# Placing the split weight tiles of a two-layer decoder trunk at 22 patterns of address distances, with four tiles of each part instead of five

## The chip, the cores and the metric

The kernel runs on one core of one Trainium2 chip. The metric is the device time of one execution in microseconds (us), as the median of several runs. Beside it there is the span of one profiled execution, from its first to its last instruction.

## The reference

A trunk of two layers runs over one sequence of 256 tokens with 2048 channels. Layer 0 mixes tokens by causal pooling, layer 1 by attention with 16 heads. Each layer ends with a gated feed-forward part of inner width 5632. Scale, shift and gate of every part come from a conditioning vector.

```python
def conv_ffn(h, w_up, conv_w, conv_b, w_down):
    u = h @ w_up                          # 2048 -> 2 * 5632
    u = causal_depthwise_conv3(u, conv_w) + conv_b
    val, gate = jnp.split(u, 2, axis=-1)
    return (jax.nn.silu(gate) * val) @ w_down

for i in range(DEPTH):                    # DEPTH = 2
    sh1, sc1, g1, sh2, sc2, g2 = jnp.split(silu(c) @ w_ada[i] + b_ada[i], 6)
    h = modulate(rmsnorm(x, norm_g[i, 0]), sh1, sc1)
    y = pool_mixer(h, ...) if i % 2 == 0 else moba_attention(h, w_qkv, w_o, rel_table)
    x = x + g1 * y
    h = modulate(rmsnorm(x, norm_g[i, 1]), sh2, sc2)
    x = x + g2 * conv_ffn(h, w_up[i], conv_w[i], conv_b[i], w_down[i])
return rmsnorm(x, final_g)
```

All data are float32.

## The kernel before

Every large weight matrix is read once, as 328 blocks of 512 rows by 512 columns, which the code calls steps. A step's block lands in one `raw` tile of [128, 2048] float32, one of five. The step has two halves of 1024 columns of that tile. For each half `w_use` has ScalarE (ACT) copy the weights into a `hi` tile of the rounded type float32r, and VectorE (DVE) subtract, `lo = w - hi`. There are HB = 5 `hi` and 5 `lo` tiles. The activations are split in the same way once (`h` for the up and the query, key and value products, `act` for the down products, `o` for the attention's output), 256 columns of rounded values beside 256 columns of remainders.

The products of a half are put out LAG = 3 halves after its split: `w_use` appends the half to `pending`, and `run_half` takes the oldest one when more than LAG are pending. The function `products` in `group_T` makes three matmuls for each 128 x 128 block of weights: `hi` by the rounded activations, `hi` by the remainders, `lo` by the rounded activations. In all of them the weights are the stationary operand (loaded by LDWEIGHTS) and the 256 columns of activations move. So a half has 4 x 2 x 3 = 24 matmuls and a step 48. Only the value projection (`v_group`) turns the roles round: there `h` is stationary and 512 columns of `hi` or `lo` move, 24 matmuls in a step. The counts are 176 steps for `w_up` (the tiles `uv` and `ug`, 8448 matmuls), 88 for `w_down` (`d`, 4224), 16 each for `k` and `q` (768 each), 16 for `v` (384), 16 for `w_o` (`wo`, 768): 14,976 matmuls with 256 columns and 384 with 512.

The first 200 us go to the conditioning vectors of the first layer (`ws` tiles, summed on DVE and TensorE) and to the pooling. The other conditioning matrices (`wa` tiles) are summed on DVE in between the steps. From event 200 on, TensorE, DVE and ACT keep the order of the program; before that a planner orders them.

Of one partition's memory the kernel takes nearly all. In the layout of the kernel before, the tile `h` starts at byte 36,864, and `act` and `o` tiles start at 156,672 and whole multiples of 8192 after it: both are multiples of 128. The `raw` tiles start at 72,640, the `hi` tiles at 113,600, the `lo` tiles at 134,080, one behind the other in steps of 8192 or 4096: all of these are 64 bytes past a multiple of 128. So in all matmuls of the steps the two operands' addresses differ by 64 bytes modulo 128, and the three operands of DVE's subtraction do not differ modulo 4096. The constants in front of the `raw` tiles set this: `starts` has room for 48 floats, of which 33 are used, and the small table `rel` lies behind the `lo` tiles.

Of the kernel before, what the change touches and what calls it, by code (L numbers as in the profile page):

```python
# [9 lines left out]
F32 = mybir.dt.float32  # L10
F32R = mybir.dt.float32r
# [6 lines left out]
P = 128  # L18
# [3 lines left out]
BUCKETS = 32  # L22
# [3 lines left out]
def bucket_starts():  # L26

    exact = BUCKETS // 2

    def bucket(n):  # L30
        if n < exact:
            return n
        big = exact + int(math.log(n / exact) / math.log(MAX_DIST / exact) * (BUCKETS - exact) + 1e-9)
        return min(big, BUCKETS - 1)

    of = [bucket(n) for n in range(4 * MAX_DIST)]
    return [next((n for n, b in enumerate(of) if b >= want), 1 << 20) for want in range(BUCKETS)]
# [19 lines left out]
def trunk(ctx: ExitStack, tc: tile.TileContext, x, c, norm_g, w_ada, b_ada, pool_w, pool_scale, w_qkv, w_o,  # L57
# [3 lines left out]
    _, S, D = x.shape  # L61
# [4 lines left out]
    H = rel_table.shape[1]  # L66
    NT = S // P
    SCALE = float(P) ** -0.5
    C = 512
# [3 lines left out]
    const = ctx.enter_context(tc.tile_pool(name="const", bufs=1))  # L73
    wp = ctx.enter_context(tc.tile_pool(name="wp", bufs=1))
# [2 lines left out]
    dram = ctx.enter_context(tc.tile_pool(name="dram", bufs=1, space=bass.MemoryType.DRAM))  # L77

    PE_BLOCKS = ((2, 5, 8, 11, 14), (3, 7, 11, 15), (2, 4, 6, 9, 11, 13, 15), (2, 5, 7, 10, 13, 15), ())
    RAW, HB, LAG, T4, PRIO = 5, 5, 3, 6, 1000  # L80

    def raw_tile(name):
        return wp.tile([P, 4 * C], F32, tag="raw", name=name, bufs=RAW)
# [4 lines left out]
    def aux(name):  # L88
        return psum.tile([P, C], F32, tag="aux", name=name, bufs=2)

    def wt(shape, tag, bufs, name, dt=F32):
        return work.tile(shape, dt, tag=tag, bufs=bufs, name=name)

    rel = wt([BUCKETS, H], "rel", 1, "rel")


    ident = const.tile([P, P], F32, name="ident")
# [310 lines left out]
    steps = []  # L408
# [259 lines left out]
    def bias_rows():  # L668

        starts = bucket_starts() + [1 << 20]  # L670
        st = const.tile([P, 48], F32, name="starts")[:, :BUCKETS + 1]
        for b, v in enumerate(starts):
            nc.gpsimd.memset(st[:, b:b + 1], float(v))
        nc.gpsimd.dma_start(rel, rel_table)
        e = wt([H, S + P], "t4", T4, "bias_e")
        nc.gpsimd.memset(e, NEG)
        for t in range(NT):
            ni = wt([P, 1], "st", 8, f"ni{t}", I32)
            nc.gpsimd.iota(ni, pattern=[[0, 1]], base=t * P, channel_multiplier=1)
            n = wt([P, 1], "st", 8, f"nf{t}")  # L680
            ve.tensor_copy(n, ni)
            ge = wt([P, BUCKETS + 1], "oh", 2, f"ge{t}")
            ve.tensor_scalar(ge, st, n, None, op0=ALU.is_le)
            oh = wt([P, BUCKETS + 1], "oh", 2, f"oh{t}")
            ve.tensor_tensor(oh[:, :BUCKETS], ge[:, :BUCKETS], ge[:, 1:], op=ALU.subtract)
            ps = aux(f"ohp{t}")
            pe.transpose(ps[:BUCKETS, :P], oh[:, :BUCKETS], ident)
            ohT = wt([BUCKETS, P], "vec", 4, f"ohT{t}")
            ve.tensor_copy(ohT, ps[:BUCKETS, :P])
            ps2 = aux(f"ohe{t}")  # L690
            pe.matmul(ps2[:H, :P], rel, ohT, start=True, stop=True)
            ve.tensor_copy(e[:, P - 1 + t * P:P - 1 + (t + 1) * P], ps2[:H, :P])
        nc.gpsimd.dma_start(bias_dram, e)
# [273 lines left out]
    def run_half():  # L967
        i, half, hi, lo = pending.pop(0)
        steps[i][3](half, hi, lo)
        if half == 1:  # L970
            for f in hooks.get(i, ()):
                f()
        h_next = ahead.pop(0) if ahead else None
        if h_next:
            h_next()
        else:
            run_tasks(2 if len(tasks) > MANY else 1)
        for _ in range(2):
            if folds:
                folds.pop(0)()  # L980
        for d in list(deferred):
            d[0] -= 1
            if d[0] <= 0:
                deferred.remove(d)
                d[1]()

    def w_use(i):
        def use(r):
            for half in range(2):
                hi = wp.tile([P, 2 * C], F32R, tag="hi", name=f"hi{i}_{half}", bufs=HB)  # L990
                lo = wp.tile([P, 2 * C], F32R, tag="lo", name=f"lo{i}_{half}", bufs=HB)
                src = r[:, half * 2 * C:(half + 1) * 2 * C]
                ac.activation(hi, src, AF.Copy)
                ve.tensor_tensor(lo, src, hi.bitcast(F32), op=ALU.subtract)
                pending.append((i, half) + tuple(t.rearrange("p (k c) -> p k c", k=2) for t in (hi, lo)))
                if len(pending) > LAG:
                    run_half()
        return use
# [47 lines left out]
    i = 0  # L1046
# [86 lines left out]
```

## Time and profile before

| | us |
|---|---|
| median of 3 runs | 2127.83 |
| lowest and highest of them | 2125.51, 2127.96 |
| the profiled execution's own time | 2123.99 |
| its span | 2121.9 |

The profiled execution was a little faster than all three of the runs, and its span leaves out 2.1 us of its own time. The mean granted TensorE clock of the execution was 0.984 of full speed. In the views, PE is the matmuls of TensorE, PEld its weight loads, DVE VectorE, ACT ScalarE. Matmuls overlap in the views, since one begins before the one ahead of it has drained, so the time that a matmul costs is the distance from its start to the next one's, and not its duration.

### The profile page before, as it was taken

The page shows a single profiled execution, that of the slowest core. Times are in us where ns is not written, and L with a number is a line of the kernel's source. Part 1 is how long each engine was busy: PE and PEld are TensorE (multiplying, and loading weights), DVE is VectorE, ACT ScalarE, POOL GpSimd, SP SyncE. Part 2 cuts the span into 40 slices and gives each one's busy share as a digit, 9 for nine tenths or more (in the row PEclk, how much of TensorE's full clock was granted, in tenths as well). Part 3 has the DMA queues.
Part 4 walks back from the last instruction along what each step waited for, and adds up shares of the span by engine and source line. Part 5 has one row for each costly group of instructions (what it writes and reads, how often), then busy time and mean ns, then how long its engine had stood idle before and what let it go on. Part 6 is the DMA issues. An engine that isn't in the chain of part 4 may idle for free.

```text
span 2121.9 us, 38504 instructions
## 1 busy us (share of the span) xinstructions
PE 2066.2 (97%) x16292; PEld 1963.9 (93%) x16292; DVE 1643.3 (77%) x2023; ACT 959.2 (45%) x1206; POOL 12.0 (1%) x64
## 2 busy tenths in 40 slices
PE   6888999999999999999999999999999999999998
PEld 2435999999999999999999999999999999999998
DVE  6877799799879998997787878779775666556655
ACT  3113633566354445444544444445443454434443
POOL 1000000000000000000000000000000000000000
PEclk9889999999999999999999999999999999999999
DMA  9999999565998988896888888578765555555551
GB/s 357 333 348 345 335 334 320 198 197 181 348 332 292 358 314 308 304 326 213 307 294 310 295 310 302 190 259 282 278 233 179 190 179 189 196 180 188 192 179 60
DMA packets 236445, 558.78 MB, mean 263 GB/s; under 512 B 9272, under 2 KB 9592, under 8 KB 221680
## 3 DMA queue, kind: packets, MB, share of 16 engines
q1 hardware_dynamic: 234800, 553.17, 74.5%
q8 instruction: 127, 2.08, 0.4%
q0 software_dynamic: 896, 2.49, 0.4%
q10 hardware_dynamic: 576, 0.67, 0.1%
q14 instruction: 46, 0.38, 0.0%
HBM read 554.17 MB, written 2.12 MB: 262 GB/s over the span
## 4 chain that ended last, share of the span: by engine, by line
PE 95%; DVE 2%; DMA 2%; ACT 1%; issue 1%; ACTq 0%; SPq 0%; DVEq 0%
PE uv L50 24%; PE ug L50 23%; PE d L50 23%; PE k L50 4%; PE wo L50 4%; PE q L50 4%; PE v L50 4%; PE row L50 2%; PE pp L50 2%; PE mods L50 1%; DVE accs L50 1%; DVE pool_room L50 1%; DMA w<-in_w_up_dram 1%; DMA ws<-in_w_ada_dram 1%; PE sc L50 0%
## 5 line engine op out<-in xcount | busy, mean ns | idle before, releaser
L50 DVE TENSOR_TENSOR lo<-w,hi 128x1024 fp32r<-128x1024 f32 x656 | 793.9, 1222 | 320.7 <-ACT hi L50 319.7
L50 ACT ACTIVATE hi<-w 128x1024 fp32r<-128x1024 f32 x656 | 682.3, 1057 | 671.9 <-PE d L50 215.8
L50 PE MATMUL uv<-h,hi 128*128 128x256 f32 x2816 | 503.8, 281 | 4.2 <-ACT h L50 4.1
L50 PE MATMUL ug<-h,hi 128*128 128x256 f32 x2816 | 501.6, 280 | 0.2 <-ACT hi L50 0.2
L50 PE MATMUL d<-act,hi 128*128 128x256 f32 x2816 | 497.5, 280 | 0.0
L50 PEld LDWEIGHTS uv<-h,hi 128*128 128x128 f32 x2816 | 433.2, 189 | 5.2 <-ACT h L50 4.9
L50 PEld LDWEIGHTS ug<-h,hi 128*128 128x128 f32 x2816 | 431.3, 188 | 0.5 <-ACT hi L50 0.5
L50 PEld LDWEIGHTS d<-act,hi 128*128 128x128 f32 x2816 | 428.9, 187 | 0.0
L50 PE MATMUL uv<-h,lo 128*128 128x256 f32 x1408 | 394.1, 280 | 0.0
L50 PE MATMUL ug<-h,lo 128*128 128x256 f32 x1408 | 393.2, 279 | 0.0
L50 PE MATMUL d<-act,lo 128*128 128x256 f32 x1408 | 390.9, 279 | 0.0
L50 PEld LDWEIGHTS uv<-h,lo 128*128 128x128 f32 x1408 | 265.8, 189 | 0.0
L50 PEld LDWEIGHTS ug<-h,lo 128*128 128x128 f32 x1408 | 264.8, 188 | 0.0
L50 PEld LDWEIGHTS d<-act,lo 128*128 128x128 f32 x1408 | 263.5, 188 | 0.0
L50 DVE SCALAR_TENSOR_TENSOR acc<-wa,cond,acc 128x2048 f32<-128x2048 f32 x105 | 246.3, 2346 | 3.5 <-DMA wa<-in_w_ada_dram 3.3
L50 DVE SCALAR_TENSOR_TENSOR accs<-ws,cond,accs 128x512 f32<-128x512 f32 (+1 forms) x179 | 157.4, 882 | 23.3 <-DMA ws<-in_w_ada_dram 12.5
L50 PE MATMUL k<-h,hi 128*128 128x256 f32 x512 | 94.0, 285 | 1.1 <-ACT h L50 1.1
L50 PE MATMUL q<-h,hi 128*128 128x256 f32 x512 | 91.4, 280 | 0.0
L50 PE MATMUL wo<-o,hi 128*128 128x256 f32 x512 | 91.1, 280 | 0.0
L50 PE MATMUL row<-ws,cond 128*1 128x512 f32 x152 | 79.5, 647 | 10.3 <-DMA ws<-in_w_ada_dram 10.3
L50 PEld LDWEIGHTS k<-h,hi 128*128 128x128 f32 x512 | 79.9, 190 | 2.3 <-ACT h L50 1.4
L50 PE MATMUL v<-hi,h 128*128 128x512 f32 x256 | 80.4, 395 | 0.0
(157 smaller groups left out, 1751.7 us busy)
## 6 DMA issues: line engine op xcount, KB each, us to landing
w<-in_w_up_dram SPq DMA_DIRECT2D x176, 1024.0 KB, 5.2
wa<-in_w_ada_dram SPq DMA_DIRECT2D x112, 1024.0 KB, 6.0
w<-in_w_down_dram SPq DMA_DIRECT2D x88, 1024.0 KB, 5.1
ws<-in_w_ada_dram SPq DMA_DIRECT2D x56, 1024.0 KB, 9.0
w<-in_w_qkv_dram SPq DMA_DIRECT2D x48, 1024.0 KB, 5.9
ws<-in_w_ada_dram SPq DMA_DIRECT2D x48, 512.0 KB, 5.8
w<-in_w_o_dram SPq DMA_DIRECT2D x16, 1024.0 KB, 5.3
pw<-in_pool_w_dram SPq DMA_DIRECT2D x4, 1024.0 KB, 9.1
```

The source lines that it names most:

```text
L50: ins = call(*args, **kwargs)
```

## The change

Each `hi` and `lo` tile gets 32 floats (128 bytes) more, and the 1024 columns in use begin 0, 32, 64 or 96 bytes into it. Which of them is set by the step's column block of 512: `n`, the block's number modulo 22, chooses a row of `SHIFTS`, which has four entries, for `hi` and `lo` of the first half and `hi` and `lo` of the second. Rows 0 to 15 are all combinations of 0 and 64. Rows 16 and 17 are 96 and 32 everywhere, rows 18 to 21 are mixtures of 96 with 64 and of 32 with 96. The tiles' names get a letter from a to v for the row. `HB` goes from 5 to 4 and `LAG` from 3 to 2. The table `rel` moves from behind the `lo` tiles to the constants, with 24 floats of room, and `starts` has 33 floats instead of 48.

```diff
-    RAW, HB, LAG, T4, PRIO = 5, 5, 3, 6, 1000
+    RAW, HB, LAG, T4, PRIO = 5, 4, 2, 6, 1000
+    SHIFTS = [tuple(64 * ((n >> b) & 1) for b in range(4)) for n in range(16)]
+    SHIFTS += [(96, 96, 96, 96), (32, 32, 32, 32), (96, 64, 96, 64), (64, 96, 64, 96), (32, 96, 32, 96), (96, 32, 96, 32)]
...
-    rel = wt([BUCKETS, H], "rel", 1, "rel")
...
-        st = const.tile([P, 48], F32, name="starts")[:, :BUCKETS + 1]
+        st = const.tile([P, BUCKETS + 1], F32, name="starts")
...
+        rel = const.tile([BUCKETS, H + 8], F32, name="rel")[:, :H]
...
-                hi = wp.tile([P, 2 * C], F32R, tag="hi", name=f"hi{i}_{half}", bufs=HB)
-                lo = wp.tile([P, 2 * C], F32R, tag="lo", name=f"lo{i}_{half}", bufs=HB)
+                n = steps[i][2] // C % len(SHIFTS)
+                hi, lo = (wp.tile([P, 2 * C + 32], F32R, tag=w, name=f"{w}{'abcdefghijklmnopqrstuv'[n]}{i}_{half}",
+                                  bufs=HB)[:, s // 4:s // 4 + 2 * C]
+                          for w, s in zip(("hi", "lo"), SHIFTS[n][2 * half:2 * half + 2]))
```

## Rows read from the trace of the kernel before

**Rows 1.** The page: busy time by engine, then the granted TensorE clock in 40 slices.

```profile
PE 2066.2 (97%) x16292; PEld 1963.9 (93%) x16292; DVE 1643.3 (77%) x2023; ACT 959.2 (45%) x1206; POOL 12.0 (1%) x64
...
PEclk9889999999999999999999999999999999999999
```

**Rows 2.** The page: the chain that ended last, shares of the span by engine.

```profile
PE 95%; DVE 2%; DMA 2%; ACT 1%; issue 1%; ACTq 0%; SPq 0%; DVEq 0%
```

**Rows 3.** The chain in order of time: start us, length us, what, instructions.

```profile
173.25 7.10 PE pp L50 x32
...
527.29 90.45 PE d L50 x768
...
1098.79 11.19 PE v L50 x48
...
1813.61 90.45 PE d L50 x768
1904.07 22.61 PE uv L50 x192
```

**Rows 4.** Two stretches of down products: length, busy us by engine, clock, DMA.

```profile
527.00:617.00 90.00, 90.00 (x767) 90.00 (x766) 73.94 (x57) 42.37 (x54) 0.00 (x0) 1.00 0.92 330
1820.00:1900.00 80.00, 80.00 (x681) 80.00 (x681) 41.87 (x44) 31.60 (x31) 0.00 (x0) 1.00 0.57 187
```

**Rows 5.** The chain in two short stretches of the attention.

```profile
1063.96 0.66 PE pt L50 x6
1064.62 2.73 PE q L50 x24
...
1068.65 2.83 PE q L50 x24
...
1190.47 2.73 PE k L50 x24
```

**Rows 6.** TensorE in order of time, value to key products: start us, length us.

```profile
982.19 0.40 PE L50 MATMUL k<-h,hi 128*128 128x256 f32 x2
982.42 0.28 PE L50 MATMUL k<-h,lo 128*128 128x256 f32 x1
982.55 0.40 PE L50 MATMUL k<-h,hi 128*128 128x256 f32 x2
982.78 0.28 PE L50 MATMUL k<-h,lo 128*128 128x256 f32 x1
982.90 0.40 PE L50 MATMUL k<-h,hi 128*128 128x256 f32 x2
```

**Rows 7.** One-column matmuls in order of time, each with its weight load.

```profile
1353.26 1.93 PE L50 MATMUL ms<-mean_c,sq 128*128 128x1 f32 x16
```

**Rows 8.** Groups by shape, DVE and ACT: busy us, mean ns, idle before.

```profile
L50 DVE TENSOR_TENSOR lo<-w,hi 128x1024 fp32r<-128x1024 f32 x656 | 793.9, 1222 | 320.7 <-ACT hi L50 319.7
...
L50 DVE TENSOR_TENSOR val<-gate,val 128x1024 f32<-128x1024 f32 x22 | 26.8, 1220 | 1.5 <-ACT gate L50 1.4
...
L50 DVE TENSOR_TENSOR pool_room<-pool_room,inv 128x1024 f32<-128x1024 f32 x4 | 4.9, 1219 | 0.0
...
L50 ACT ACTIVATE hi<-w 128x1024 fp32r<-128x1024 f32 x656 | 682.3, 1057 | 671.9 <-PE d L50 215.8 <-PE ug L50 176.9 <-PE uv L50 173.5
...
L50 ACT ACTIVATE sq<-xT 128x1024 f32<-128x1024 f32 x4 | 4.2, 1053 | 28.6 <-DVE xT L50 28.6
```

**Rows 9.** What TensorE waited for: us in total, times, longest us.

```profile
PE ug L50 <- ACT hi L50: 0.2, 1, 0.2
```

**Rows 10.** ACT, DVE and TensorE in order of time, around one half of `wo`.

```profile
1321.66 1.06 ACT L50 ACTIVATE hi<-w 128x1024 fp32r<-128x1024 f32 x1 [1.72 <-PE wo L50]
...
1321.95 1.22 DVE L50 TENSOR_TENSOR lo<-w,hi 128x1024 fp32r<-128x1024 f32 x1
...
1325.12 0.40 PE L50 MATMUL wo<-o,hi 128*128 128x256 f32 x2
```

## The prediction

> **What bounds the kernel now.** I read the page first. TensorE is busy 97% of the span at full granted clock nearly throughout [rows 1], and the chain that ended last is 95% TensorE [rows 2]. Since busy time of overlapping matmuls says little, the chain in order of time comes next, for its pieces give the distance from matmul to matmul: 768 down products in 90.45 us, 192 up products in 22.61 us [rows 3], both 117.8 ns each. The 14,976 matmuls with 256 columns take 14,976 x 117.8 = 1764 us of the 2121.9, so one nanosecond more or less on each is worth 15 us.
>
> Is 117.8 ns set by something that the change touches? The two stretches of down products have DVE busy 82% and 52% of the time and the DMA share at 0.92 and 0.57, and 767 matmuls in 90 us and 681 in 80 are the same distance [rows 4]. So it is set inside TensorE. There are two marks to hold it against. One-column matmuls, where the weight load alone sets the pace, follow each other at about (1.93 - 0.25) / 15 = 112 ns, with 0.25 us off for the last one's own length, an estimate [rows 7]. And in two stretches of 24 matmuls, on the same operands at the same distance of addresses, the matmuls are faster: 2.73 us where the next half takes 2.83 [rows 5], which is 4.2 ns less on each. Both come after short transposes, the first visibly so. So the matmul's own reading and the weight load beside it get in each other's way, by an amount that depends on how the two stand in time to each other, and a stream that has once begun at one pace keeps it. The value products, with 512 columns, take 11.19 / 48 = 233.1 ns [rows 3], where 512 columns at 2.4 GHz would take 213.3: a loss of 20 ns against 117.8 - 106.7 = 11.1 ns with 256 columns. The plain float32 matmuls of the pooling, 7.10 / 32 = 222 ns for 256 columns [rows 3], run at half the column rate and show no sign of a loss that could be told apart. That is all the trace holds: every matmul of the steps has its operands 64 bytes apart modulo 128, so no row shows another distance.
>
> **The change, part by part.** First the addresses that it makes. `starts` shrinks from 192 bytes to 160 (33 floats, in units of 32 bytes) and `rel` adds 96, so `raw` moves up by 64 to 72,704, a multiple of 128. Tiles of 4224 bytes are 33 x 128, so `hi` and `lo` without a shift start at multiples of 128, as `h`, `act` and `o` still do. A shift is thus the distance itself. The row of shifts is the column block's number modulo 22: up products use all 22 rows (384 matmuls each), down, query and output products rows 0 to 3, key products 4 to 7, value products 8 to 11. Counting `hi` twice and `lo` once in each triple, 5344 of the 14,976 matmuls keep the 64 bytes, 7712 have 0, and 1920 have 32 or 96. In halves that hold 6624 matmuls, 2208 triples, `hi` and `lo` have different shifts, so that the distance changes twice in each triple: 4416 changes.
>
> *DVE and ACT.* The subtraction, all operands at one address modulo 128, takes 1222 ns, the gate's product of two tiles at one address modulo 128 takes 1220, and the pooling's product, whose operands lie 64 bytes apart, 1219; ACT's copy takes 1057, its squaring from a tile 64 bytes off 1053 [rows 8]. These differ by less than 1% over the distances that occur, and both engines stand beside TensorE's work. Cost 0; were 1% added to the 794 and 682 us, the idle time of the two would take it in.
>
> *Tiles and lag.* With four tiles a split waits until the products of four halves before are through, not five: it can start one half, 24 x 117.8 = 2.83 us, later, and nothing else holds it. Behind a copy that waits on ACT stand the convolution's and the gate's tasks, and DVE's subtraction waits for it; TensorE waits last. The cover now: TensorE has waited for a split only 0.2 us in all [rows 9]. From the start of each half's first product and the end of its subtraction I find, in the last 596 of the 656 halves, 13 with less than 2.83 us between them, the least 1.62. All shortfalls added, neighbours counted once, make 5.8 us: the upper end. But most of the 13 began late for a load or for work before them on DVE, and such a split does not move. The clearest that does: its copy waits for TensorE and starts at 1321.66, the subtraction ends at 1323.17, and the product begins at 1325.12 [rows 10], so 1.95 us of cover against 2.83, a loss of 0.9. I take 1 us, range 0 to 6. The load behind a split is late by the same 2.83 us at most; five `raw` tiles with the DMA share at 0.57 to 0.92 [rows 4] cover that. The moved table costs nothing: the same transfer on the same queue, long before it is used.
>
> *A new distance that stays.* For 7712 matmuls at 0 and 1920 at 32 or 96, the trace bounds the price from two sides: the shorter pace of [rows 5], -4.2 ns, and a loss as large as that of the value products on a 256-column matmul, 106.7 + 20 = 126.7, so +8.9 ns. On 9632 matmuls that is -40 to +86 us. I take 0, because 117.8 is what all entries but two fell into, after interruptions of every kind.
>
> *Distances that change within a triple.* The nearest row is the passage from value to key products, where operands change roles: the first triple takes 982.19 to 982.55, 0.36 us, the one after it 0.35 [rows 6]. At that resolution a change costs 0 to 7 ns. I take the half, 3.5 ns: 4416 x 3.5 = 15 us, range 0 to 31.
>
> The sum: 1 + 0 + 15 + 0 = 16 us. On the profiled execution that is 2124.0 + 16 = 2140 us. The median of the runs shown is 3.8 us above that execution, and I forecast the median: 2127.8 + 16 = 2144 us, 0.8% slower.
>
> The Trainium skill speaks against any effect of the distance: its page "SBUF — State Buffer", section "Who interferes with whom", gives TensorE two independent read ports, one for the moving operand and one for the weight load, and says that it never waits on anyone. By that only the 1 us for the tiles would be left, 2129 us; the trace does not bear it out fully, since two speeds stand side by side on the same addresses [rows 5]. Its page "TensorE: Matmul & The Clock Gate", section "Back-to-back issue gap", has 262 cycles for 256 columns, an estimate of 109 ns; the trace's 117.8 does not agree, so there is a loss that an address could lengthen or shorten.
>
> **The rivals.** *The distance does nothing.* The loss may be one of time alone: the two speeds on equal addresses [rows 5] speak for that, and so does that the steps' distances are constant and the speed nevertheless is not. Then 2127.8 + 1 = 2129 us, within the bound of 0.2% (4 us), which is about what a measurement can tell here from no change. Against it: the interference is between two reads of one memory.
>
> *Distance 0 or a mixture leads into the shorter pace.* The pace that saves 4.2 ns exists [rows 5]. If distance 0 alone leads to it, 7712 x 4.2 = 32 us go: 2097 us, or 2112 with the 15 us of changes; if all streams fall into it, 62 us, 2067. It becomes faster than before from about (16 + 4) / 4.2 ns = 4800 matmuls on if the changes cost their 15 us. Against it: it is rare, 2 stretches of 24.
>
> *Distance 0 is a bad one.* If a weight load at the moving operand's own address modulo 128 loses as much as the value products do, 7712 x 8.9 = 69 us come on top: 2144 + 69 = 2213. The down products would show it most, as they use rows 0 to 3 alone.
>
> **How the numbers follow.** Changes within a triple cost something, up to the bound of 31 us and with small losses at new distances: 0.45, with a range of its own from 2133 to 2165. Distance 0 bad, in part or wholly, 2165 to 2213: 0.12. Nothing from the distance: 0.16. The shorter pace: 0.27. So slower 0.57, same 0.16, faster 0.27. The range leaves out the deeper third of the faster case, below 2085, and the end of the bad one, above 2200.
>
> **What would show it.** The letters in the tiles' names give each row of shifts its own lines, so pieces of the chain such as 192 matmuls of one up block compare directly with 22.61 us. Right would be: rows a, d, m and p (one distance in a half) near 117.8 ns, rows with unequal `hi` and `lo`, most of all s to v, some 2 ns above. Waits of TensorE for `hi` or `lo` should stay under 6 us in all. DVE's 1222 and ACT's 1057 ns should stand for all letters. What would make me wrong: a block at 113 ns, down products off 117.8 ns at all, or a DVE that is slower at some distance and so late for TensorE.

## The result, and the profile after

The changed kernel takes 2137.9 us (median of 4 runs, 2134.46 to 2140.51), the kernel before beside it 2127.1 (4 runs, 2125.51 to 2127.96): a ratio of 1.0051 with an interval of [1.0033, 1.0068], 10.8 us slower. The forecast was 2144 us, 16 us slower. So direction and size fit, but the sum behind them doesn't: the term that was to bring 15 us brings nothing, and the one put at 1 us brings ten.

The page of the kernel after: busy time by engine, the clock, and four of its groups (busy us, mean ns, idle before).

```profile
PE 2074.7 (97%) x16292; PEld 1967.8 (92%) x16292; DVE 1643.2 (77%) x2023; ACT 959.5 (45%) x1206; POOL 12.0 (1%) x64
...
PEclk8888999999999999999999999999999999999999
...
L50 PE MATMUL d<-act,hia 128*128 128x256 f32 x704 | 126.8, 282 | 0.6 <-ACT hia L50 0.6
...
L50 PE MATMUL d<-act,hid 128*128 128x256 f32 x704 | 124.2, 280 | 0.0
L50 DVE TENSOR_TENSOR loa<-w,hia 128x1024 fp32r<-128x1024 f32 x76 | 91.7, 1222 | 42.1 <-ACT hia L50 41.9
...
L50 ACT ACTIVATE hia<-w 128x1024 fp32r<-128x1024 f32 x76 | 79.3, 1057 | 91.1 <-PE d L50 42.8
```

DVE and ACT work as in [rows 8], 1222 and 1057 ns. TensorE is still busy all the time as in [rows 1], and the down products of letters a and d differ by 2.6 us of busy time over the same 704 matmuls. A busy time of overlapping matmuls can't say what that is worth; the chain in order of time can (start us, length us, what, instructions):

```profile
1262.12 2.26 DVE acc L50
1264.38 1.15 DVE lol L50
...
1265.57 5.83 PE v L50 x24
...
1646.57 22.63 PE uv L50 x192
1669.20 21.76 PE ug L50 x192
...
1713.42 22.55 PE ug L50 x192
...
1826.52 90.80 PE d L50 x768
...
1940.04 23.01 PE ug L50 x192
...
2031.02 22.41 PE ug L50 x192
```

Each piece of 192 matmuls is one up block, and so one row of shifts; against the 22.61 us of [rows 3] these are e 22.63, p 21.76, q 22.55, t 23.01 and v 22.41: from 113.3 to 119.8 ns where everything used to take 117.8. So the distance between the operands' addresses does set TensorE's pace, and both ways. Yet the 768 down products (rows a to d) take 90.80 us instead of 90.45, almost the same, because their four rows in part make up for each other.

That can be seen with every matmul's start taken from the trace. The table gives the mean distance from start to start in the halves whose `hi` and `lo` shifts are the given ones, over all letters:

```
hi, lo shift, bytes   0,0     0,64    64,0    64,64   32,32   96,96   32,96   96,32   64,96   96,64
ns                    119.14  117.60  117.40  115.45  119.09  117.24  118.84  116.65  119.0   118.21
```

Distance 0 costs 1.4 ns against the 117.77 of before, distance 64 gives back 2.3, and all 256-column matmuls of the steps together have 117.87. The 115.45 is a mean of two: of the 80 such halves that the records show whole, 39 stand at 113.3, 38 at 117.3 to 119, and three between.

What TensorE waits for on account of a split (us in total, times, longest us), which was one wait of 0.2 us before [rows 9]:

```profile
PE k L50 <- DVE loh L50: 1.4, 2, 1.2
...
PE d L50 <- DVE lob L50: 1.2, 2, 0.9
...
PE d L50 <- DVE loa L50: 1.1, 1, 1.1
PE v L50 <- DVE loj L50: 0.9, 1, 0.9
PE v L50 <- DVE lok L50: 0.9, 1, 0.9
PE v L50 <- DVE lol L50: 0.8, 1, 0.8
PE k L50 <- DVE lof L50: 0.8, 2, 0.6
...
PE d L50 <- ACT hia L50: 0.6, 1, 0.6
```

That is 7.7 us. One such wait stands in the chain above: the pooled sum `acc` of a conditioning matrix runs 2.26 us on DVE, the split `lol` comes behind it, and the value products begin when it is done. So at this point two readings were open: the loss is the lateness of splits, and the distances come out at nothing; or the distances cost, and the waits are their result.

### The profile page after: what moved, and what is told of

Its sections match the earlier page's. It is cut to its first block, busy times and chain, and to the rows that moved or that the text cites. A ratio compares the mean times of both kernels' runs of the same rounds, so it can differ in the third digit from the quotient of the medians.

```text
span 2136.1 us, 38497 instructions
## 1 busy us (share of the span) xinstructions
PE 2074.7 (97%) x16292; PEld 1967.8 (92%) x16292; DVE 1643.2 (77%) x2023; ACT 959.5 (45%) x1206; POOL 12.0 (1%) x64
## 5 line engine op out<-in xcount | busy, mean ns | idle before, releaser
L50 PE MATMUL d<-act,hia 128*128 128x256 f32 x704 | 126.8, 282 | 0.6 <-ACT hia L50 0.6
L50 PE MATMUL d<-act,hib 128*128 128x256 f32 x704 | 127.3, 283 | 0.0
L50 PE MATMUL d<-act,hic 128*128 128x256 f32 x704 | 125.9, 281 | 0.0
L50 PE MATMUL d<-act,hid 128*128 128x256 f32 x704 | 124.2, 280 | 0.0
L50 DVE TENSOR_TENSOR loa<-w,hia 128x1024 fp32r<-128x1024 f32 x76 | 91.7, 1222 | 42.1 <-ACT hia L50 41.9
L50 ACT ACTIVATE hia<-w 128x1024 fp32r<-128x1024 f32 x76 | 79.3, 1057 | 91.1 <-PE d L50 42.8
L50 PEld LDWEIGHTS d<-act,hib 128*128 128x128 f32 x704 | 109.2, 191 | 0.0
L50 PEld LDWEIGHTS d<-act,hia 128*128 128x128 f32 x704 | 108.3, 190 | 0.8 <-ACT hia L50 0.8
L50 PEld LDWEIGHTS d<-act,hic 128*128 128x128 f32 x704 | 108.2, 189 | 0.0
L50 PEld LDWEIGHTS d<-act,hid 128*128 128x128 f32 x704 | 107.7, 189 | 0.0
L50 PE MATMUL d<-act,lob 128*128 128x256 f32 x352 | 99.4, 284 | 1.2 <-DVE lob L50 1.2
L50 PE MATMUL d<-act,loc 128*128 128x256 f32 x352 | 98.8, 282 | 0.0
```

The costliest lines, as they stand in the source:

```text
L50: ins = call(*args, **kwargs)
```

## The experiments

Times are medians; each ratio is to the kernel before, run on the same chip beside it (2122.7 us, 2122.7 and 2123.7 in the three series).

### Tiles and lag alone

Kernel before, with four tiles and lag 2 and no change of a distance:

```diff
-    RAW, HB, LAG, T4, PRIO = 5, 5, 3, 6, 1000
+    RAW, HB, LAG, T4, PRIO = 5, 4, 2, 6, 1000
```

> The kernel before with four tiles of each part and a lag of two, and no new distances. Theory A (the whole loss of the change is waiting for splits): TensorE waits some 8 to 10 us for hi and lo in the steps, the pace stays 117.8 ns everywhere, and the time is 8 to 12 us above before, 0.4% to 0.55%. Rival B (the loss comes from the distances, the waits are given back elsewhere): under 3 us above before.

Measured: 2133.1 us (6 runs), ratio 1.0045 [1.0029, 1.0062], so 10.4 us, the whole loss of the change. Its waits for splits:

```profile
PE d L50 <- DVE lo L50: 2.5, 3, 1.1
PE v L50 <- DVE lo L50: 2.5, 3, 0.8
PE k L50 <- DVE lo L50: 2.1, 4, 1.2
...
PE d L50 <- ACT hi L50: 0.6, 1, 0.6
```

7.7 us again, with the pace at 117.76 ns. The new distances are not needed for the loss. Which of the two numbers makes it? Kernel before with five tiles and only the lag changed:

```diff
-    RAW, HB, LAG, T4, PRIO = 5, 5, 3, 6, 1000
+    RAW, HB, LAG, T4, PRIO = 5, 5, 2, 6, 1000
```

> The kernel before with a lag of two and still five tiles. If the fourth tile's loss is the cause of the waits, the time of before within 3 us; if the lag, which puts each split behind the tasks of one half more, is the cause, 6 to 10 us above before as with four tiles.

Measured: 2133.7 us (6 runs), ratio 1.0048 [1.0035, 1.0061], 11.1 us. The fifth tile comes back and nothing is gained by it. Its waits for splits are 5.7 us:

```profile
PE v L50 <- DVE lo L50: 2.5, 3, 0.8
PE k L50 <- DVE lo L50: 2.1, 4, 1.2
PE d L50 <- DVE lo L50: 1.1, 1, 1.1
```

DVE of the kernel with lag 2, in order of time, and the value product that waits:

```profile
1103.81 0.69 DVE L50 TENSOR_TENSOR sm<-sc,bias 128x512 f32<-128x512 f32 x1 [0.52 <-PE sc L50]
...
1105.40 1.22 DVE L50 TENSOR_REDUCE mx<-sm 128x4 f32<-128x1024 f32 x1
...
1107.53 2.35 DVE L50 SCALAR_TENSOR_TENSOR acc<-wa,cond,acc 128x2048 f32<-128x2048 f32 x1
1109.79 2.35 DVE L50 TENSOR_TENSOR lo<-w,hi 128x1024 fp32r<-128x1024 f32 x2
```
```profile
1111.06 0.50 PE L50 MATMUL v<-lo,h 128*128 128x512 f32 x1 [0.84 <-DVE lo L50]
```

The softmax and one `acc` (`sm`, `mx` and `acc` in the view) keep DVE from 1103.81 to 1109.79, 6 us without a split. Two halves of value products are 2 x 12 x 233 ns = 5.6 us, and that is what lag 2 has in hand; three halves, 8.4 us, cover it. The subtraction is not held by a buffer. It stands where the program puts it, and its products come one half sooner.

In the records the first step's matmul starts at 200.7 us before and at 203.7 and 205.5 in these two, but at 196.3 to 199.3 in three of the four-tile kernels below, so the late start doesn't come with the lag each time. From that matmul to the end, before has 1921.2 us, lag 2 has 1927.6 and four tiles with lag 2 have 1930.4. So of the 11.2 us between the spans of lag 2 and of before, 6.4 lie behind that matmul, and the 5.7 us of waits nearly make them up; the other 4.8 lie ahead of it, and no run shows whether the lag causes them. Up to 3 us may be the fourth tile's; the medians don't part them.

### One distance for all

The changed kernel with row p, 64 everywhere:

```diff
-                n = steps[i][2] // C % len(SHIFTS)
+                n = 15
```

> The changed kernel with 64 bytes in all shifts, so that every distance is that of before, at tiles in steps of 4224 bytes with raw tiles at multiples of 128. Rival B (the layout makes the 113.3 ns that the group with 64 in all shifts showed): 113.3 ns throughout and some 55 to 65 us less than the changed kernel, near 2077 us. Theory A (a stream takes one of two paces when it begins and keeps it as long as the distance stays): 117.8 ns nearly throughout, as before, and the time of the four-tile kernel, near 2137 us.

Measured: 2074.75 us (4 runs), ratio 0.9773 [0.9754, 0.9791]. This is 48 us faster than before, with the late splits still in it (8.9 us of waits). A piece of the chain that answers to the last two of [rows 3]:

```profile
1775.96 87.04 PE d L50 x768
1863.00 21.76 PE uv L50 x192
```

87.04 / 768 = 113.3 ns. Of the 618 halves that could be read, 573 go at 113.3 and 40 at 117.8. What is remarkable is that before, too, has 64 bytes modulo 128 everywhere, and goes at 117.8. Now row a, 0 everywhere (`n = 0` in the same line):

> The changed kernel with 0 in all shifts. If the pace depends on the distance as the halves at 0 of the changed kernel have it (119.1 ns), the 14,976 matmuls take (119.1 - 117.9) x 14,976 = 18 us more than the changed kernel, near 2156 us, and DVE and ACT stay at 1222 and 1057 ns. If the distance does nothing by itself: the changed kernel's time within 3 us.

Measured: 2156.3 us (4 runs), ratio 1.0150 [1.0126, 1.0174].

```profile
1840.47 91.57 PE d L50 x768
1932.05 22.89 PE uv L50 x192
```

22.89 / 192 = 119.2 ns; its halves stand at 118.5 or 120. Which of the two is set by the tile: the tiles lie 4224 bytes apart, so modulo 256 the distance is 0 and 128 by turns, and of the halves that the records show whole and without a pause (two starts 200 ns or more apart) the 253 at 0 have 119.8 ns in the mean, the 267 at 128 have 118.6. So the pace goes by the distance modulo 256 and not only modulo 128. Distance 0 is the worst one tried in a whole kernel, by 1.5 ns over both, not by the 8.9 of the rival.

### Changes of the distance

The kernel before with a fifth tile that lies 64 bytes further, so that one half in five has distance 0 modulo 128 and the others keep theirs; modulo 128 no triple is mixed. These lines take the place of the two that make `hi` and `lo` in the kernel before:

```diff
+                m = 2 * i + half
+                j, kick = m % HB, m % (HB * 1) == HB - 1
+                hi, lo = (wp.tile([P, 2 * C + (32 if j == HB - 1 else 0)], F32R, tag=f"{w}{j}",
+                                  name=f"{w}{'k' if kick else ''}{i}_{half}", bufs=1)[:, 16 * kick:16 * kick + 2 * C]
+                          for w in ("hi", "lo"))
```

> The kernel before with five tiles and a lag of three, in which the fifth tile of each part begins 64 bytes further, so that one half in five has distance 0. Theory A: a stream at 64 that follows one at 0 mostly takes 113.3 ns; with four fifths at 113.3 to 114 and one fifth at 119 to 120 ns the mean is 114.5 to 115.3, and the time 35 to 50 us below before, 2077 to 2092 us. Rival B (the pace belongs to the layout or to the group, not to how a stream begins): 117.8 ns at 64 and 119 at 0, mean 118.0, 4 us above before.

Measured: 2127.4 us (10 runs), ratio 1.0028 [1.0015, 1.0041]. The halves at 64 go at 117.81 ns and those at 0 at 119.55, so a half at 0 between them doesn't move the others to the shorter pace; that hope is gone. Then the reverse: every triple mixed, `hi` at 64 and `lo` at 0 (`n = 5` in the changed kernel). The 4992 triples of the 256-column products have two changes each, 9984 against the 4416 of the change.

> The changed kernel with 64 bytes for hi and 0 for lo in every half, so that the distance changes twice in each triple and is otherwise the same all along. My prediction's price of 3.5 ns for a change: 117.8 + 2 x 3.5 / 3 = 120.1 ns, 34 us above the changed kernel, near 2172 us. If a change has no price of its own and each matmul goes by the distances beside it, as in the changed kernel's halves of this kind (117.4 ns): 7 us below it, near 2131 us.

Measured: 2124.3 us (10 runs), ratio 1.0011 [0.9999, 1.0023], with lag 2 and four tiles in it.

```profile
1819.26 89.87 PE d L50 x768
1909.13 22.47 PE uv L50 x192
```

22.47 / 192 = 117.0 ns, and 117.14 over all steps. At 3.5 ns a change it would have been 35 us more than its parts; instead the mixed triples are quicker than the 117.77 of before. Against that pace, which is what the prediction reckoned from, a change within a triple has no price. Against the shorter pace there may be one: (2 x 113.65 + 119.25) / 3 = 115.5 ns would be the mean of the last two kernels, 1.6 ns below, or 2.5 ns for each change. That can't be told from a pace of its own that such triples have, and here too the halves differ by the tile: 117.9 ns with 64 and 0 modulo 256, 116.3 with 192 and 128.

### Why before goes at 117.8 and the all-64 kernel at 113.3

In the kernel before the tiles lie 4096 bytes apart, so the distance is 192 bytes modulo 256 in every half. In the all-64 kernel they lie 4224 apart, and it alternates between 64 and 192. First the same kernel, lag 2 and four tiles, with steps of 4096, so that it is 64 modulo 256 in all halves (`rel` and `starts` as in the change; `gap(n)` puts `n` unused floats there, once):

```diff
+                gap(16)
                 hi = wp.tile([P, 2 * C], F32R, tag="hi", name=f"hi{i}_{half}", bufs=HB)
+                gap(128)
                 lo = wp.tile([P, 2 * C], F32R, tag="lo", name=f"lo{i}_{half}", bufs=HB)
+                gap(112)
```

> The all-64 kernel with its hi and lo tiles in steps of 4096 bytes instead of 4224, everything else where it was: raw at multiples of 128, the first hi and lo tiles at the same bytes, four tiles, a lag of two. The distance is 64 modulo 256 in every half and never changes. Theory C: 117.8 ns in most halves and the time of the four-tile kernel, 2133 us. Rival D, or a rival for which 64 modulo 256 is good and 192 bad: 113.3 ns and the time of the all-64 kernel, 2075 us.

Measured: 2092.7 us (4 runs), ratio 0.9872 [0.9853, 0.9891], between the two answers expected. Both paces are in it, on the same addresses:

```profile
1269.60 70.67 PE wo L50 x600
...
1419.18 21.76 PE ug L50 x192
```

70.67 / 600 = 117.8 and 21.76 / 192 = 113.3. Then the kernel before with only its fifth tile 128 bytes further, five tiles and lag 3 (lines in the same place):

```diff
+                j = (2 * i + half) % HB
+                last = j == HB - 1
+                hi = wp.tile([P, 2 * C + 32 * last], F32R, tag=f"hi{j}", name=f"hi{'x' * last}{i}_{half}", bufs=1)[:, 32 * last:]
+                lo = wp.tile([P, 2 * C], F32R, tag=f"lo{j}", name=f"lo{'x' * last}{i}_{half}", bufs=1)
```

> The kernel before, five tiles and a lag of three, in which only the fifth tile of each part lies 128 bytes further modulo 256, so that the distance modulo 256 changes twice in five halves and stays 64 modulo 128. Theory C (a stream at 117.8 ns goes over to 113.3 where the distance changes by 128 bytes, and then stays): 113.3 to 114 ns in most halves, 55 to 65 us less than before, 2058 to 2070 us, with no waits for hi or lo. Rival D (the 113.3 ns of the all-64 kernel comes from where raw tiles lie or from the 512 bytes between hi and lo): 117.8 ns and the time of before within 4 us.

Measured: 2071.3 us (4 runs), ratio 0.9758 [0.9745, 0.9772], a mean pace of 114.2 ns. The moment at which a stream goes over is to be seen:

```profile
248.09 5.65 PE uv L50 x48
253.74 5.47 PE ug L50 x48
259.21 10.88 PE uv L50 x96
```

After an interruption by short `mods` products at 245 us TensorE goes at 117.8, in the next step it passes to 113.3, and there it stays until the next interruption. It also falls back where the moving operand goes from `h` to `act` or from `act` to `h`, which in this layout lie 128 apart modulo 256: at all 10 passages without a pause that begin at 113.3. One of them, with the block behind it:

```profile
600.61 22.30 PE uv L50 x192
622.91 21.76 PE ug L50 x192
```

22.30 / 192 = 116.1 ns, and then 113.3. In the all-64 kernel, where `h` and `act` lie at one address modulo 256, all 9 such passages stay at 113.3.

The last two have five tiles and lag 3. In the first all tiles lie 128 bytes further than before, a constant 64 modulo 256; in the second the tiles 2 and 4 do, so that 192 and 64 take turns. Beside that, the second has its `hi` and `lo` tiles in alternating order, as the kernel with one half in five at 0 had them, whose other halves went at 117.81, and `ones` is cut to 32 columns for the room. The first diff is the constant one's, the second, in the same place as before, that with turns:

```diff
+                if i + half == 0:
+                    wp.tile([P, 32], F32, tag="gap1", name="gap1", bufs=1)
...
+                if i + half == 0:
+                    wp.tile([P, 32], F32, tag="gap2", name="gap2", bufs=1)
```
```diff
+                j = (2 * i + half) % HB
+                gap = 32 if j else 0
+                hi = wp.tile([P, 2 * C + gap], F32R, tag=f"hi{j}", name=f"hi{'x' * (j % 2)}{i}_{half}", bufs=1)[:, gap:]
+                lo = wp.tile([P, 2 * C], F32R, tag=f"lo{j}", name=f"lo{'x' * (j % 2)}{i}_{half}", bufs=1)
```

> The kernel before with hi and lo tiles all 128 bytes further, so that the distance is 64 modulo 256 everywhere and constant. Theory C (the pace is drawn when a stream begins anew and then kept): a mixture of long stretches at 113.3 and at 117.8 ns, as in the kernel with steps of 4096, mean 114 to 117 ns, 2070 to 2112 us. If the distance modulo 256 sets the pace outright: 113.3 ns throughout, 2060 us. If only changes do anything: 117.8 ns and the time of before.

> The kernel before, five tiles and a lag of three, with the second and fourth tiles of each part 128 bytes further, so that the distance is 192, 64, 192, 64, 192 bytes modulo 256 from half to half, and with h and act at one address modulo 256. Theory C in its sharper form (a change from 192 to 64 ends the 117.8 ns, a change from 64 to 192 or none leaves the pace as it is): the falls back at each passage between up and down products in the kernel with one such tile are gone, 113.4 to 113.8 ns in the mean, and 5 to 11 us less than that kernel, 2060 to 2066 us. If which tiles are shifted does not matter beyond the first: the same time as that kernel, 2071 us.

Measured: constant 64 takes 2079.45 us (4 runs), ratio 0.9792 [0.9776, 0.9808]; taking turns 2061.1 us (5 runs), ratio 0.9709 [0.9695, 0.9723]. The constant one:

```profile
522.23 90.45 PE d L50 x768
...
666.56 78.96 PE d L50 x696
745.52 21.76 PE uv L50 x192
```

117.8 ns in the first layer's first down block, and after the small `modc` product at 666.4 us 113.4 and then 113.3 until 941.9 us. A stream at constant distance mostly keeps the pace that it has until something interrupts it. The one with turns:

```profile
510.29 87.04 PE d L50 x768
597.33 21.76 PE uv L50 x192
```

113.3 ns from the first down block on. The joints of two halves can be counted, over the three kernels in which the distance changes between 64 and 192 (64 everywhere, fifth tile 128 further, turns), where the records show both halves whole, no pause lies between them and the moving operand stays the same. From 192 to 64 a stream at 117.8 went over to 113.3 in 31 of 45 cases, from 64 to 192 in 2 of 14, with no change in 4 of 66, and one at 113.3 stayed there in 1432 of 1435. In the kernel before a stream at 117.8 stayed there at all 542 such joints. So a change from 192 to 64 is the kick that before never gets. Before's constant 192 has the long pace, apart from the two short stretches in [rows 5].

A constant distance of 64 isn't the same as one of 192 either. Over joints with a pause a stream at 117.8 came back at 113.3 in 2 of 26 cases before, and in 15 of 21 in the two kernels with 64 modulo 256 throughout. So those get the shorter pace at interruptions, and 192 seldom does.

That pace and lag are all there is can be tested on the sum: 14,976 matmuls by the pace's difference from 117.77 ns, and 10.4 us, measured by the first experiment, where the lag is 2 and the tiles are four, against what was measured.

| kernel | pace, ns | pace term, us | lag term, us | sum | measured |
|---|---|---|---|---|---|
| the change | 117.87 | +1.5 | +10.4 | +11.9 | +10.8 |
| 64 everywhere | 113.65 | -61.7 | +10.4 | -51.3 | -48.0 |
| 0 everywhere | 119.25 | +22.2 | +10.4 | +32.6 | +33.6 |
| half in five at 0 | 118.09 | +4.8 | 0 | +4.8 | +4.7 |
| `hi` 64, `lo` 0 | 117.14 | -9.4 | +10.4 | +1.0 | +1.6 |
| 64 mod 256, lag 2 | 115.08 | -40.3 | +10.4 | -29.9 | -30.0 |
| fifth tile 128 further | 114.17 | -53.9 | 0 | -53.9 | -51.4 |
| 64 mod 256, lag 3 | 114.81 | -44.3 | 0 | -44.3 | -44.2 |
| 192 and 64 in turns | 113.64 | -61.9 | 0 | -61.9 | -62.5 |

All nine agree within 3.3 us.

## Why the prediction came out near, and where it failed

*Tiles and lag, "I take 1 us, range 0 to 6": mis-sized, 10 to 11 us by the medians, 6.4 of them placed by the record of lag 2 alone.* It asked what a split loses when its buffer comes free 2.83 us later, and found that most of the close ones "began late for a load or for work before them on DVE, and such a split does not move". For the fourth tile this can stand (some 3 us at most, by the records). But the lag is a second, separate change: the products come one half sooner while those splits stay behind the softmax and the `acc` on DVE, and it is just those that TensorE now waits for. "The clearest that does" move, at 1325 us, is not among the waits, and it was misread: by [rows 10] the copy that starts at 1321.66 ends at 1322.72, so the subtraction that begins at 1321.95 is not its own but that of a half whose copy ran before, and whose products begin at 1327.24, 4.1 us after it. The step counted the cover of the buffer and not the cover of the order.

*A new distance that stays, "I take 0": +0.1 ns, about 1.5 us net, but by compensation.* At distance 0 it costs 1.4 ns and at 64 gives back 2.3 on the mean. The lower bound, "the shorter pace of [rows 5]", was the mark to follow: it is a state that streams at 64 bytes modulo 128 can have, and the rows' 2.73 / 24 = 113.8 ns is near its 113.3. The reason for 0, that 117.8 is "what all entries but two fell into", held for one distance only, 192 modulo 256, and the text counted distances modulo 128.

*Distances that change within a triple, 15 us: nil against before's pace.* The row behind it resolved 0 to 7 ns a change and the half was taken without a reason for a price. With the three terms at 10.4, 1.5 and 0 the sum is 11.9; the forecast of 16 was close because a term too large stood beside one too small, and that is luck.

*DVE and ACT, 0:* right, as the groups of the page after show.

*The rivals.* "The distance does nothing" is refuted, although its time (2129) is nearer than it deserves. "Distance 0 is a bad one" is right in direction and a sixth of the size. "Distance 0 or a mixture leads into the shorter pace" had the right state and the wrong cause: no mixture leads there; distance 64 does, most surely where it alternates modulo 256.

*The test written down, "rows a, d, m and p near 117.8, s to v some 2 ns above":* a 119.2, d 117.2, m 117.6, p 113.5; s 118.3, t 119.4, u 118.9, v 116.7. The block at 113 ns that "would make me wrong" is there, it is p. The waits for splits, which "should stay under 6 us in all", are 7.7.

*The Trainium skill.* Its page "SBUF — State Buffer", section "Who interferes with whom", has TensorE's two read ports independent and TensorE never waiting on anyone; by that no distance could matter, but 0 everywhere and 64 everywhere differ by 81.5 us with the same instructions in the same order. The measurement decides.

What stays open is the mechanism. Matmuls and weight loads run beside each other ([rows 1] has the two busy for 97% and 93% of the span), and in the changed kernel the distance from one start to the next goes by the distance between the next matmul's weights and the moving operand (mean 118.7 ns at 0 modulo 128, 116.7 at 64) a little more than by that of the matmul's own weights (118.4 and 117.0). That fits two reads of one memory that meet or miss each other, but no run shows the memory's parts. Why a 192-to-64 change succeeds 31 times in 45 and not always, and what decides at an interruption, wasn't settled.

## What to carry to other kernels

Where TensorE is the bound and its products stream at one pace, measure that pace in the chain and try the relative addresses of its two operands as one would try a tile size: here a layout alone, for 512 bytes of a partition's room, takes 2.9% off the time (the kernel with turns, 2061 us, is the one to keep). Probe one distance for a whole kernel, for a kernel that mixes them shows a mean in which gains and losses cancel, and a stream's past carries over into the next block. And price the lag of a software pipeline by what stands in the queue between two splits, not by the number of buffers.

## What the hardware showed that was not expected

Two paces on the same addresses, 113.3 and 117.8 ns, each held for hundreds of microseconds (the constant-64 kernel above). In the changed kernel the granted clock fell to half (0.51, the level of 1.2 GHz) for 3.4 us right after three waits for splits between 687 and 693 us; the four-tile kernel has the same three waits at 688 to 693 us and no such drop, and the kernels with 64 and with 0 everywhere have one, at 674 and 696 us. Windows of the kernel after (length, busy us by engine, clock, DMA share):

```profile
693.40:696.90 3.50, 3.50 (x19) 3.50 (x18) 3.50 (x4) 0.07 (x1) 0.00 (x0) 0.51 1.02 400
697.00:706.00 9.00, 9.00 (x78) 9.00 (x78) 8.63 (x7) 4.07 (x4) 0.00 (x0) 1.00 1.01 391
```

19 matmuls in 3.5 us where full clock has 78 in 9: 184 ns each instead of 115, about 1.3 us lost.
